# Memory attention of a hybrid encoder layer: three engines in written order, twelve rounds instead of ten

## The chip, the core and the metric

The kernel runs on one core of a Trainium2 chip. The metric is the device time of one execution in microseconds (us). Engines are named as the profile names them: PE (matmuls), DVE (vector), ACT (scalar), POOL (GpSimd) and SP, whose queue issues the DMAs.

## The reference

One encoder layer over 1024 tokens of width 1024. After a norm and one wide projection it has three branches: latent attention with 8 heads ("MLA"), a short convolution, and cross-attention into 256 memory tokens with 4 heads of width 128. Each branch is gated, sent through a matrix, weighted by a sigmoid, and the sum goes through the output matrix. The change is in the third branch alone:

```python
mkv = (rmsnorm(mem, mem_norm_g) @ w_mkv).reshape(B, M, N_HEADS_MEM, 2 * MEM_HEAD_DIM)
m_k, m_v = split_cols(mkv, (MEM_HEAD_DIM, MEM_HEAD_DIM))
mq = rmsnorm(q_mem.reshape(B, S, N_HEADS_MEM, MEM_HEAD_DIM), mem_q_g)
m_k = rmsnorm(m_k, mem_k_g)
s = jnp.einsum('bshd,bmhd->bhsm', mq, m_k).astype(jnp.float32) * (MEM_HEAD_DIM ** -0.5)
p = jax.nn.softmax(s, axis=-1).astype(m_v.dtype)
o_mem = jnp.einsum('bhsm,bmhd->bshd', p, m_v).reshape(B, S, MEM_WIDTH) * jax.nn.silu(g_mem)
```

## The kernel before, in words

Every float32 product is three matmuls: each operand is split into a high and a low part (`mm3`, lines 107 to 111). The wide projection is "dense" work: a generator (`dense`, line 478 on) that issues one matmul per `pull`, 48 for each block of weights, and PE is fed with it wherever a stage would leave PE waiting. A weight block is loaded by SP, split by POOL (`whi` at line 74, `wlo` at line 80) and used by PE. `self.parts` says whether a block is split in one piece or in four quarters that are spread over the 48 pulls of the block before. The dense results go through `sg` (ACT, line 620) and a store `d_r`.

Memory attention (`mem_attn`, line 792 on) goes over 8 blocks of 128 tokens. For a block: `q` projects and normalizes (24 matmuls; `hsq`, `hst`, `qn`), `turn` copies the two 16-bit planes of the result on DVE (`pl`, line 85) and transposes each with a DMA (`plt`, line 86); `qt` puts the planes together again on ACT (`pw`, line 90) and splits into `qh` (ACT) and `ql` (DVE); `sm` computes 12 score matmuls, the maximum (line 830), four exponentials (line 834), the division on POOL (line 836), and turns the probabilities by the same way of planes; `t` puts them together and splits them into `pth` (ACT) and `ptl` (DVE); `o` does the value products of two blocks in two groups of 12 matmuls, multiplies by the gate that a DMA has brought (`gm`, line 861), splits on POOL (`omh`, `oml`) and stores. The tile `gm` has one buffer, so that a gate is loaded only after the split of the gate before.

The MLA loop (`mla`, line 925 on) follows: 64 rounds of scores, maximum (line 957), exponential, planes, transposes, splitting and products, with dense pulls between. There DVE, ACT and POOL run in the order in which the code is written (`manual_schedule`), and so does PE in both stages. In memory attention DVE, ACT and POOL are ordered by the scheduler of the language, which places an instruction by its own estimate of times; SP is ordered so in both stages. The pulls of the MLA loop are what is left up to a fixed total (`r_end - rest - self.pulled`), spread evenly over 70 rounds.

Of the kernel before, what the change touches and what calls it, by code (L numbers as in the profile page):

```python
# [9 lines left out]
F32 = mybir.dt.float32  # L10
F32R = mybir.dt.float32r
# [3 lines left out]
ALU = mybir.AluOpType  # L15
# [3 lines left out]
P = 128  # L19
S = 1024  # L20
D = 1024
TB = S // P
KT = D // P
M = 256
# [3 lines left out]
HM, DM = 4, 128  # L28
EPS = 1e-6
MAGIC = 12582912.0  # L30
NB = 256
# [31 lines left out]
class K:  # L63
# [728 lines left out]
    def mem_attn(self, st, wq, swq):  # L792
        tc, nc, a, d = self.tc, self.nc, self.a, self.d
        v, ps = nc.vector, self.ps
        mt = M // P
        sc = DM ** -0.5
        wk = self.pool(st, "wk3", bufs=2, side="right")
        QN, QT, PR, PT = {}, {}, {}, {}

        def q(tb):  # L800
            ts = slice(tb * P, (tb + 1) * P)
            pq = ps.tile([P, 512], F32, name="mm", bufs=3)
            for kt in range(KT):
                self.mm3(pq, self.hh[:, kt, ts], self.hl[:, kt, ts], wq[0][:, kt, :], wq[1][:, kt, :], kt == 0, kt == KT - 1)
            QN[tb] = wk.tile([P, HM, DM], F32, name="qn", bufs=1)
            self.head_norm(wk, QN[tb], pq.rearrange("p (h d) -> p h d", d=DM), HM, DM)
            QN[tb] = turn(QN[tb].rearrange("p h d -> p (h d)"), 512)

        def turn(x, n):
            pl = wk.tile([P, 2, n], U16, name="pl%d" % n, bufs=1)  # L810
            plt = wk.tile([P, 2, n // P, P], U16, name="plt%d" % n, bufs=1)
            self.planes(x, pl, plt)
            return plt

        def back(plt, n):
            w = wk.tile([P, S // P, P], F32, name="pw", bufs=1)[:, :n // P]
            self.words(w, plt)
            return w

        def qt(tb):  # L820
            QT[tb] = (wk.tile([P, HM, P], F32R, name="qh"), wk.tile([P, HM, P], F32R, name="ql"))
            self.evac(back(QN.pop(tb), 512), *QT[tb], self.mg[:, 0:1])

        def sm(tb):
            qh, ql = QT.pop(tb)
            s = ps.tile([P, HM, M], F32, name="s")
            for h in range(HM):
                self.mm3(s[:, h, :], qh[:, h, :], ql[:, h, :], self.mk[0][:, h, :], self.mk[1][:, h, :], True, True)
            mx = wk.tile([P, 4 * HM], F32, name="mx4", bufs=3)
            v.tensor_reduce(out=mx[:, 0:HM], in_=s, axis=AX.X, op=ALU.max)  # L830
            v.tensor_scalar_mul(mx[:, HM:2 * HM], mx[:, 0:HM], -sc)
            p = wk.tile([P, HM, M], F32, name="p", bufs=2)
            for h in range(HM):
                nc.scalar.activation(out=p[:, h, :], in_=s[:, h, :], func=AF.Exp, scale=sc, bias=mx[:, HM + h:HM + h + 1], accum_out=mx[:, 2 * HM + h:2 * HM + h + 1])
            v.reciprocal(mx[:, 3 * HM:], mx[:, 2 * HM:3 * HM])
            nc.gpsimd.tensor_tensor(out=p, in0=p, in1=mx[:, 3 * HM:].unsqueeze(2).broadcast_to([P, HM, M]), op=ALU.mult)
            PR[tb] = turn(p.rearrange("p h m -> p (h m)"), S)

        def t(tb):
            blk, j = divmod(tb, NB // P)  # L840
            js = slice(j * P, (j + 1) * P)
            w = back(PR.pop(tb), S)
            if j == 0:
                PT[blk] = [[wk.tile([P, 2, mt, NB], F32R, name="pt" + x) for x in "hl"] for _ in range(2)]
            for g in range(2):
                self.evac(w[:, 4 * g:4 * g + 4].rearrange("p (h k) c -> p h k c", h=2), PT[blk][g][0][:, :, :, js], PT[blk][g][1][:, :, :, js])

        def o(blk):
            bs = slice(blk * NB, (blk + 1) * NB)
            pts = PT.pop(blk)  # L850
            for g in range(2):
                gs = slice(2 * g, 2 * g + 2)
                gm = wk.tile([P, 2, NB], F32, name="gm", bufs=1)
                nc.sync.dma_start(gm, d["gm"][:, gs, bs])
                po = ps.tile([P, 2, NB], F32, name="po")
                for hh in range(2):
                    h = 2 * g + hh
                    for k in range(mt):
                        vh, vl = (x[:, k, h * DM:(h + 1) * DM] for x in self.mv)
                        self.mm3(po[:, hh, :], vh, vl, pts[g][0][:, hh, k, :], pts[g][1][:, hh, k, :], k == 0, k == mt - 1)  # L860
                v.tensor_tensor(out=gm, in0=po, in1=gm, op=ALU.mult)
                oh = wk.tile([P, 2, NB], F32R, name="omh", bufs=1)
                ol = wk.tile([P, 2, NB], F32R, name="oml", bufs=1)
                self.split(gm, oh, ol)
                nc.sync.dma_start(d["omh"][:, gs, bs], oh.bitcast(F32))
                nc.sync.dma_start(d["oml"][:, gs, bs], ol.bitcast(F32))
                self.pull(6)

        for i in range(TB + 2):
            n = 8 if i < TB else 16  # L870
            if i < TB:
                q(i)
            if i == TB - 1:
                swq.close()
                self.open_heads()
            if 0 <= i - 1 < TB:
                qt(i - 1)
            if i == TB:
                with tc.issue_after(self.turned):
                    self.load_q(0)  # L880
                    self.load_head(0)
                    self.load_q(1)
            self.pull(n)
            if 0 <= i - 1 < TB:
                sm(i - 1)
            self.pull(n)
            if 0 <= i - 2 < TB:
                t(i - 2)
            self.pull(n)
            if i > 2 and i % 2:  # L890
                o((i - 3) // 2)

    def open_heads(self):
        self.HD = {}
# [306 lines left out]
```

## Time and profile before

| what | before |
|---|---|
| runs, us | 1170.7, 1175.63, 1172.23; median 1172.23 |
| the profiled execution's own time, us | 1169.31 |
| its span from first to last instruction, us | 1167.6 |
| PE busy over the span | 1125.0 us (96%) |
| DVE, ACT, POOL busy over the span | 721.0, 549.3, 565.8 us |
| mean granted clock of PE | 0.993 of full speed |

The times in rows of the trace count from the first instruction of the profiled execution. A row of the timeline gives the start, the duration, engine and line, operation, result<-source and shapes, how many instructions are merged in it (x), and in brackets the idle time of the engine just ahead with what ended it. Matmuls are pipelined, so that the distance between two starts, not the duration, is what one costs. Memory attention runs from 427 to 586 us, the MLA loop from there to 905 us.

### The profile page before, as it was taken

To read this page: it belongs to the slowest core of one execution; us is meant where nothing else is said; L and a number is where in the kernel's file an instruction comes from. 1 tells how busy PE (TensorE), PEld (TensorE's weight loads), DVE (VectorE), ACT (ScalarE), POOL (GpSimd) and SP (SyncE) were. 2 spreads that over 40 slices of the span, in tenths; PEclk is the share of its full clock that TensorE was granted. 3 is DMA by queue.
4 is the path that set the end of the run, shared out by engine and by line. 5 is a ranking of instruction groups with operands and counts; after the bars stand their busy time and mean duration, and the time that the engine had idled before them with its cause. 6 is when DMAs were issued, how large, how long until landed. Compare 5 with 4: busy or idle time off the path is not lost.

```text
span 1167.6 us, 15350 instructions
## 1 busy us (share of the span) xinstructions
PE 1125.0 (96%) x5458; PEld 945.8 (81%) x5458; DVE 721.0 (62%) x1084; ACT 549.3 (47%) x821; POOL 565.8 (48%) x478
## 2 busy tenths in 40 slices
PE   7999999899999999989899999999999999999998
PEld 7998787678888888777778878888888878888887
DVE  6997686343325443556269999999999204656121
ACT  6546575511011105555468878788788302322000
POOL 4456475343324552344447685876785823233200
PEclk8999999999999999999999999999999999999999
DMA  8427999933232333454979999998997598545241
GB/s 297 150 100 178 241 229 250 259 106 107 73 118 81 127 98 101 108 139 114 266 189 222 215 217 216 217 244 204 232 202 161 167 409 304 160 144 173 98 150 49
DMA packets 284589, 207.75 MB, mean 178 GB/s; under 512 B 201632, under 2 KB 253472, under 8 KB 284320
## 3 DMA queue, kind: packets, MB, share of 16 engines
q1 hardware_dynamic: 284512, 206.76, 65.8%
q8 instruction: 43, 0.70, 0.2%
q14 instruction: 34, 0.28, 0.1%
HBM read 108.14 MB, written 50.33 MB: 136 GB/s over the span
## 4 chain that ended last, share of the span: by engine, by line
PE 41%; DVE 22%; DMA 13%; issue 11%; ACT 7%; POOL 4%; SPq 1%; ACTq 0%; DVEq 0%; POOLq 0%
DVE pl L85 8%; PE mm L526 5%; PE mm L530 5%; PE mm L528 5%; DVE mx L957 5%; DMA plt<-pl 5%; PE mm L713 4%; PE mm L715 4%; PE mm L711 4%; PE mm L109 3%; PE mm L110 3%; PE mm L111 3%; DVE ptl L982 2%; PE pm L760 2%; DMA plt<-plq 2%
## 5 line engine op out<-in xcount | busy, mean ns | idle before, releaser
L526 PE MATMUL mm<-hh,whi 128*128 128x512 f32 x672 | 263.7, 392 | 3.5 <-DVE sg L603 3.5
L530 PE MATMUL mm<-hh,wlo 128*128 128x512 f32 x672 | 261.9, 392 | 1.2 <-POOL wlo L80 1.2
L528 PE MATMUL mm<-hl,whi 128*128 128x512 f32 x672 | 262.8, 391 | 0.0
L90 ACT COPY pw<-plt 128x1024 uint16<-128x1024 uint16 (+1 forms) x160 | 198.4, 1305 | 36.5 <-DMA plt<-pl 33.4
L74 POOL TENSOR_SCALAR whi<-wraw 128x256 fp32r<-128x256 f32 (+1 forms) x107 | 107.2, 1002 | 199.5 <-PE pm L760 76.4
L80 POOL TENSOR_TENSOR wlo<-wraw,whi 128x256 fp32r<-128x256 f32 (+1 forms) x108 | 173.5, 1606 | 9.8 <-PE tr L318 1.6
L526 PEld LDWEIGHTS mm<-hh,whi 128*128 128x128 f32 x672 | 126.6, 188 | 30.5 <-DVE sg L603 4.8
L530 PEld LDWEIGHTS mm<-hh,wlo 128*128 128x128 f32 x672 | 126.7, 189 | 27.9 <-POOL wlo L80 1.6
L528 PEld LDWEIGHTS mm<-hl,whi 128*128 128x128 f32 x672 | 126.6, 188 | 25.8
L85 DVE COPY pl<-p 128x1024 uint16<-128x1024 uint16 x144 | 132.7, 961 | 20.0 <-ACT p L960 9.3
L978 POOL TENSOR_SCALAR pth<-pw 128x1024 fp32r<-128x1024 f32 x64 | 80.8, 1262 | 91.2 <-ACT pw L90 91.2
L952 PE MATMUL s<-k,q 96*128 96x512 f32 x384 | 99.5, 394 | 2.3 <-ACT p L960 1.6
L960 ACT ACTIVATE p<-s,mx 128x1024 f32<-128x1024 f32 x64 | 71.5, 1118 | 58.5 <-DVE mx L957 58.3
L982 DVE TENSOR_TENSOR ptl<-pw,pth 128x1024 fp32r<-128x1024 f32 x64 | 94.5, 1477 | 6.8 <-POOL pth L978 6.4
L952 PEld LDWEIGHTS s<-k,q 96*128 96x128 f32 x384 | 71.7, 188 | 20.5 <-ACT p L960 3.1
L957 DVE TENSOR_REDUCE mx<-s 128x1 f32<-128x1024 f32 x64 | 77.2, 1206 | 0.4
L688 ACT ACTIVATE sg<-sg 128x1024 f32<-128x1024 f32 x24 | 25.5, 1062 | 90.1 <-DMA sg<-d_r 88.8
L391 ACT COPY pw<-plt 96x512 uint16<-96x512 uint16 x64 | 43.8, 771 | 27.5 <-DMA plt<-plq 21.8
L620 ACT ACTIVATE sg<-mm,small 128x512 f32<-128x512 f32 x48 | 32.9, 687 | 37.7 <-PE mm L530 25.5
L718 DVE TENSOR_TENSOR acc<-mm,sg 128x512 f32<-128x512 f32 x16 | 10.9, 689 | 52.1 <-PE mm L715 40.3
L76 ACT CAST whi<-wraw 128x1024 fp32r<-128x1024 f32 x9 | 9.5, 1051 | 68.3 <-PE mm L528 66.8
L996 PE MATMUL po<-pth,v 128*128 128x256 f32 x256 | 38.4, 293 | 0.0
(322 smaller groups left out, 2338.5 us busy)
## 6 DMA issues: line engine op xcount, KB each, us to landing
wraw<-in_w_feat SPq DMA_DIRECT2D x48, 512.0 KB, 4.2
d_r<-sg SPq DMA_DIRECT2D x24, 512.0 KB, 3.9
sg<-d_r SPq DMA_DIRECT2D x24, 512.0 KB, 3.8
d_k<-qkt SPq DMA_DIRECT2D x32, 192.0 KB, 3.0
d_q<-qkt SPq DMA_DIRECT2D x32, 192.0 KB, 3.0
q<-d_q SPq DMA_DIRECT2D x32, 192.0 KB, 3.4
wraw<-in_w_br SPq DMA_DIRECT2D x12, 512.0 KB, 4.3
k<-d_k SPq DMA_DIRECT2D x12, 384.0 KB, 5.6
```

Source lines behind the costliest of these rows:

```text
L74: nc.gpsimd.tensor_scalar(out=hi, in0=raw, scalar1=1.0, scalar2=1.0, op0=ALU.mult, op1=ALU.mult)
L80: e.tensor_tensor(out=lo, in0=raw, in1=hi.bitcast(F32), op=ALU.subtract)
L85: self.nc.vector.tensor_copy(pl[:, x], _halves(src, x))
L90: self.nc.scalar.copy(_halves(out, x), plt[:, x])
L526: mm(o, w1, self.hh[:, k, c], start=k == 0, stop=False)
L528: mm(o, w1, self.hl[:, k, c], start=False, stop=False)
L530: mm(o, w2, self.hh[:, k, c], start=False, stop=k == KT - 1)
L952: nc.tensor.matmul(s[:, c], q[:, qi, ts], k[:, ki, c], start=s_, stop=e_)
L957: v.reduce_max(out=mx[:, 1:2], in_=s, axis=AX.X, negate=True)
L960: nc.scalar.activation(out=p, in_=s, func=AF.Exp, bias=mx[:, 1:2], accum_out=mx[:, 2:3])
L978: nc.gpsimd.tensor_scalar(out=parts(i)[0], in0=p, scalar1=1.0, scalar2=1.0, op0=ALU.mult, op1=ALU.mult)
L982: v.tensor_tensor(out=lo, in0=PW.pop(i), in1=hi.bitcast(F32), op=ALU.subtract)
```

## The change

`sm` is divided into `scores` and `soft`, `q` into `q` and `norm`, `o` into `o` and `fin`. Memory attention now fixes DVE, ACT and POOL to written order too, with weight splits in quarters (`self.parts = 4`). A block's scores come two rounds after its projection (before: one), its `t` three (two), and the products of blocks 2b and 2b+1 in round 2b+5 (2b+3), so that 12 rounds stand where 10 stood. `pw` gets a second buffer, `po` a second, `p` loses one. The gate's DMA is written directly ahead of its multiplication instead of ahead of the products. The pulls of the stage are 360 (15 half blocks) instead of 336; the MLA loop gets 24 fewer.

```diff
+        man.enter_context(tc.manual_schedule(engines={E.DVE, E.Activation, E.Pool}))
+        self.parts = 4
...
-            w = wk.tile([P, S // P, P], F32, name="pw", bufs=1)[:, :n // P]
+            w = wk.tile([P, S // P, P], F32, name="pw", bufs=2)[:, :n // P]
...
-            p = wk.tile([P, HM, M], F32, name="p", bufs=2)
+            p = wk.tile([P, HM, M], F32, name="p", bufs=1)
...
+        def o(blk, g):
+            pts = PT[blk]
+            po = ps.tile([P, 2, NB], F32, name="po", bufs=2)
...
+        def fin(blk, g, po):
             bs = slice(blk * NB, (blk + 1) * NB)
...
+            gs = slice(2 * g, 2 * g + 2)
+            gm = wk.tile([P, 2, NB], F32, name="gm", bufs=1)
+            nc.sync.dma_start(gm, d["gm"][:, gs, bs])
+            v.tensor_tensor(out=gm, in0=po, in1=gm, op=ALU.mult)
...
-        for i in range(TB + 2):
-            n = 8 if i < TB else 16
+        LAST = TB + 3
+        for i in range(LAST + 1):
+            n = 8 if i < TB else 14
+            blk = (i - 5) // 2 if i >= 5 and i % 2 else None
+            if 0 <= i - 2 < TB:
+                scores(i - 2)
+                soft(i - 2)
+            self.pull(n)
             if i < TB:
                 q(i)
...
             if 0 <= i - 1 < TB:
                 qt(i - 1)
-            if i == TB:
+            if blk is not None:
+                po = [o(blk, 0)]
+            self.pull(n // 2)
+            if blk is not None:
+                po.append(o(blk, 1))
+            self.pull(n - n // 2)
+            if blk is not None:
+                fin(blk, 0, po[0])
+            if 0 <= i - 3 < TB:
+                t(i - 3)
+            if 0 <= i - 2 < TB:
+                PR[i - 2] = turn(PR[i - 2].rearrange("p h m -> p (h m)"), S)
+            if i < TB:
+                norm(i)
+            if i == TB + 1:
                 with tc.issue_after(self.turned):
                     self.load_q(0)
                     self.load_head(0)
                     self.load_q(1)
             self.pull(n)
-            if 0 <= i - 1 < TB:
-                sm(i - 1)
-            self.pull(n)
-            if 0 <= i - 2 < TB:
-                t(i - 2)
-            self.pull(n)
-            if i > 2 and i % 2:
-                o((i - 3) // 2)
+            if blk is not None:
+                fin(blk, 1, po[1])
+        man.close()
```

Two places where the order moves. The first is DVE in the middle of the stage, in the kernel before: the first two gate multiplications (L861) and what stands around them (L830 maximum, L96 `ptl`, L85 planes, L788 to L790 the norm).

```order
L861 TENSOR_TENSOR gm<-po,gm 128x512
L835 RECIPROCAL mx_4083<-mx_4083 128x4
L99 SCALAR_TENSOR_TENSOR ql<-pw,small,qh 128x512
L85 COPY pl_4093<-p 128x1024 x2
L788 TENSOR_REDUCE hst<-hsq 128x4
L861 TENSOR_TENSOR gm<-po,gm 128x512
L96 TENSOR_TENSOR ptl<-pw,pth 128x4x128
L104 TENSOR_SCALAR hst<-hst 128x4
L96 TENSOR_TENSOR ptl<-pw,pth 128x4x128
L830 TENSOR_REDUCE mx_4254<-s 128x4
L790 TENSOR_TENSOR qn<-mm,hst 128x512
```

The same place in the changed kernel (L840 the maximum, L873 the gate, other lines as before), one whole round from maximum to maximum:

```order
L840 TENSOR_REDUCE mx_4232<-s 128x4
L841 TENSOR_SCALAR mx_4232<-mx_4232 128x4
L845 RECIPROCAL mx_4232<-mx_4232 128x4
L99 SCALAR_TENSOR_TENSOR ql<-pw,small,qh 128x512
L873 TENSOR_TENSOR gm<-po,gm 128x512
L96 TENSOR_TENSOR ptl<-pw,pth 128x4x128 x2
L85 COPY pl_4341<-p 128x1024 x2
L788 TENSOR_REDUCE hst<-hsq 128x4
L104 TENSOR_SCALAR hst<-hst 128x4
L790 TENSOR_TENSOR qn<-mm,hst 128x512
L85 COPY pl_4355<-qn 128x512 x2
L873 TENSOR_TENSOR gm<-po,gm 128x512
```

Every round now has the same sequence: one block's maximum, the next block's `ql`, the previous block's `ptl`, its successor's planes and the newest block's norm follow one another, and the parts of different blocks no longer overtake each other.

The second place is SP's queue at the end of the stage, in the kernel before, from the planes of the second last block of probabilities on (`q`, `k`, `v` are the first loads of the MLA loop):

```order
L86 DMA_TRANSPOSE plt_4675<-pl_4674 128x8x128 x2
L866 DMA d_oml<-oml 128x2x256
L854 DMA gm<-d_gm 128x2x256
L923 DMA q<-d_q 96x2x256
L910 DMA k<-d_k 96x2048
L911 DMA v<-d_v 128x8x128
L923 DMA q<-d_q 96x2x256
```

In the changed kernel, from the planes of the last block on:

```order
L86 DMA_TRANSPOSE plt_4872<-pl_4871 128x8x128
L877 DMA d_omh<-omh 128x2x256
L86 DMA_TRANSPOSE plt_4872<-pl_4871 128x8x128
L878 DMA d_oml<-oml 128x2x256
L949 DMA q<-d_q 96x2x256
L936 DMA k<-d_k 96x2048
L937 DMA v<-d_v 128x8x128
L949 DMA q<-d_q 96x2x256
L872 DMA gm<-d_gm 128x2x256
L622 DMA d_r<-sg 128x1024
L486 DMA wraw<-in_w_feat 128x1024
```

The gate of the second group of blocks 4 and 5 stood ahead of the four MLA loads and now stands behind them; the last transposes stood behind them and now stand ahead. On DVE that gate's multiplication is followed by the last block's `ptl` and then the two gates of blocks 6 and 7, with the MLA loop's first maximum (L983) next:

```order
L873 TENSOR_TENSOR gm<-po,gm 128x512
L96 TENSOR_TENSOR ptl<-pw,pth 128x4x128 x2
L873 TENSOR_TENSOR gm<-po,gm 128x512 x2
L983 TENSOR_REDUCE mx<-s 128x1
L85 COPY pl<-p 128x1024 x2
```

In this sequence the last block's `ptl` comes behind one gate and the MLA loop's first maximum behind two more.

## Rows read from the trace of the kernel before

**Rows 1.** Windows: us; busy us (x) of PE, PEld, DVE, ACT, POOL; clock; DMA share; GB/s
```profile
427.00:586.00 159.00, 147.44 (x722) 122.89 (x720) 77.33 (x114) 78.03 (x145) 65.39 (x46) 0.99 0.55 145
507.00:510.00 3.00, 3.00 (x10) 2.41 (x9) 2.76 (x4) 2.97 (x5) 1.48 (x3) 0.58 0.00 0
```
**Rows 2.** Waits of PE in the stage: total us, times, longest us
```profile
PE s L109 <- ACT qh L98: 3.4, 2, 2.2
PE po L109 <- ACT pth L95: 3.1, 1, 3.1
```
**Rows 3.** Timeline of PE: first and last of 24 projection, of 12 score matmuls
```profile
427.07 0.39 PE L109 MATMUL mm<-wqh,hh 128*128 128x512 f32 x1
...
432.28 0.39 PE L111 MATMUL mm<-wqh,hl 128*128 128x512 f32 x1
...
457.52 0.28 PE L109 MATMUL s<-mkh,qh 128*128 128x256 f32 x1
...
458.82 0.28 PE L111 MATMUL s<-mkh,ql 128*128 128x256 f32 x1
```
**Rows 4.** Timeline of DVE and ACT: the pieces of one block's way
```profile
433.49 0.68 DVE L788 TENSOR_REDUCE hst<-hsq 128x4 f32<-128x512 f32 x1
...
436.23 0.76 DVE L85 COPY pl<-qn 128x512 uint16<-128x512 uint16 x2
...
460.99 0.76 DVE L85 COPY pl<-qn 128x512 uint16<-128x512 uint16 x2
...
468.89 1.28 DVE L85 COPY pl<-p 128x1024 uint16<-128x1024 uint16 x2
...
542.79 2.67 ACT L90 COPY pw<-plt 128x1024 uint16<-128x1024 uint16 x2 [3.83 <-DMA plt<-pl]
...
546.14 1.29 DVE L96 TENSOR_TENSOR ptl<-pw,pth 128x512 fp32r<-128x512 f32 x2 [0.50 <-ACT pth L95]
...
547.61 0.47 ACT L834 ACTIVATE p<-s,mx 128x256 f32<-128x256 f32 x1 [0.40 <-DVE mx L831]
...
549.43 1.42 ACT L90 COPY pw<-plt 128x512 uint16<-128x512 uint16 x2
...
550.88 0.72 ACT L98 ACTIVATE qh<-pw,small 128x512 fp32r<-128x512 f32 x1
```
**Rows 5.** Timeline: planes of a projected block, and when ACT has them back
```profile
532.73 0.75 DVE L85 COPY pl<-qn 128x512 uint16<-128x512 uint16 x2
...
535.71 0.78 ACT L90 COPY pw<-plt 128x512 uint16<-128x512 uint16 x1 [0.25 <-DMA plt<-pl]
```
**Rows 6.** Timeline of POOL and DVE: a weight split beside the plane copies
```profile
537.02 2.38 POOL L80 TENSOR_TENSOR wlo<-wraw,whi 128x1024 fp32r<-128x1024 f32 x1
...
537.10 3.46 DVE L85 COPY pl<-p 128x1024 uint16<-128x1024 uint16 x2 [2.01 <-POOL p L836]
```
**Rows 7.** Timeline: the last two gates, the MLA loop's first scores and maximum
```profile
581.26 0.69 DVE L861 TENSOR_TENSOR gm<-po,gm 128x512 f32<-128x512 f32 x1 [1.06 <-PE po L111]
...
586.21 3.06 PE L952 MATMUL s<-k,q 96*128 96x512 f32 x12 [0.78 <-ACT sg L620]
...
587.48 0.69 DVE L861 TENSOR_TENSOR gm<-po,gm 128x512 f32<-128x512 f32 x1 [5.53 <-DMA gm<-d_gm]
588.09 1.22 DVE L957 TENSOR_REDUCE mx<-s 128x1 f32<-128x1024 f32 x1
```
**Rows 8.** DMA issues from 425 to 592 us: count, KB each, median us to landing
```profile
gm<-d_gm SPq DMA_DIRECT2D x8, 256.0 KB, 3.0
...
v<-d_v SPq DMA_DIRECT2D x2, 512.0 KB, 8.1
```
**Rows 9.** The MLA loop: a window, a DVE group with its idle time, a PE wait
```profile
630.00:870.00 240.00, 235.01 (x1220) 196.70 (x1219) 231.26 (x286) 197.58 (x235) 176.97 (x169) 1.00 0.98 217
...
L957 DVE TENSOR_REDUCE mx<-s 128x1 f32<-128x1024 f32 x47 | 56.7, 1207 | 0.4
...
PE po L993 <- DVE o L1017: 5.5, 9, 1.4
```

More of the change, by code (lines that the diff above doesn't have):

```diff
@@ L797, in mem_attn, with norm @@
         wk = self.pool(st, "wk3", bufs=2, side="right")
-        QN, QT, PR, PT = {}, {}, {}, {}
+        PQ, QN, QT, PR, PT = {}, {}, {}, {}, {}
+        E = mybir.EngineType
+        man = st.enter_context(ExitStack())
+        man.enter_context(tc.manual_schedule(engines={E.DVE, E.Activation, E.Pool}))
+        self.parts = 4
         def q(tb):
             ts = slice(tb * P, (tb + 1) * P)
-            pq = ps.tile([P, 512], F32, name="mm", bufs=3)
+            pq = PQ[tb] = ps.tile([P, 512], F32, name="mm", bufs=3)
             for kt in range(KT):
                 self.mm3(pq, self.hh[:, kt, ts], self.hl[:, kt, ts], wq[0][:, kt, :], wq[1][:, kt, :], kt == 0, kt == KT - 1)
-            QN[tb] = wk.tile([P, HM, DM], F32, name="qn", bufs=1)
-            self.head_norm(wk, QN[tb], pq.rearrange("p (h d) -> p h d", d=DM), HM, DM)
-            QN[tb] = turn(QN[tb].rearrange("p h d -> p (h d)"), 512)
+        def norm(tb):
+            qn = wk.tile([P, HM, DM], F32, name="qn", bufs=1)
+            self.head_norm(wk, qn, PQ.pop(tb).rearrange("p (h d) -> p h d", d=DM), HM, DM)
+            QN[tb] = turn(qn.rearrange("p h d -> p (h d)"), 512)
         def turn(x, n):
@@ L822, in qt, with scores, soft @@
             self.evac(back(QN.pop(tb), 512), *QT[tb], self.mg[:, 0:1])
-        def sm(tb):
+        def scores(tb):
             qh, ql = QT.pop(tb)
-            s = ps.tile([P, HM, M], F32, name="s")
+            s = PR[tb] = ps.tile([P, HM, M], F32, name="s")
             for h in range(HM):
                 self.mm3(s[:, h, :], qh[:, h, :], ql[:, h, :], self.mk[0][:, h, :], self.mk[1][:, h, :], True, True)
+        def soft(tb):
+            s = PR[tb]
             mx = wk.tile([P, 4 * HM], F32, name="mx4", bufs=3)
@@ L836, in sm @@
             nc.gpsimd.tensor_tensor(out=p, in0=p, in1=mx[:, 3 * HM:].unsqueeze(2).broadcast_to([P, HM, M]), op=ALU.mult)
-            PR[tb] = turn(p.rearrange("p h m -> p (h m)"), S)
+            PR[tb] = p
         def t(tb):
@@ L846, in t @@
                 self.evac(w[:, 4 * g:4 * g + 4].rearrange("p (h k) c -> p h k c", h=2), PT[blk][g][0][:, :, :, js], PT[blk][g][1][:, :, :, js])
-        def o(blk):
-            bs = slice(blk * NB, (blk + 1) * NB)
[L850 to L867, printed above, removed]
@@ L869, in mem_attn @@
-        for i in range(TB + 2):
-            n = 8 if i < TB else 16
+        def o(blk, g):
+            pts = PT[blk]
+            po = ps.tile([P, 2, NB], F32, name="po", bufs=2)
+            for hh in range(2):
+                h = 2 * g + hh
+                for k in range(mt):
+                    vh, vl = (x[:, k, h * DM:(h + 1) * DM] for x in self.mv)
+                    self.mm3(po[:, hh, :], vh, vl, pts[g][0][:, hh, k, :], pts[g][1][:, hh, k, :], k == 0, k == mt - 1)
+            return po
@@ new lines, in fin @@
+        def fin(blk, g, po):
+            bs = slice(blk * NB, (blk + 1) * NB)
+            gs = slice(2 * g, 2 * g + 2)
+            gm = wk.tile([P, 2, NB], F32, name="gm", bufs=1)
+            nc.sync.dma_start(gm, d["gm"][:, gs, bs])
+            v.tensor_tensor(out=gm, in0=po, in1=gm, op=ALU.mult)
+            oh = wk.tile([P, 2, NB], F32R, name="omh", bufs=1)
+            ol = wk.tile([P, 2, NB], F32R, name="oml", bufs=1)
+            self.split(gm, oh, ol)
+            nc.sync.dma_start(d["omh"][:, gs, bs], oh.bitcast(F32))
+            nc.sync.dma_start(d["oml"][:, gs, bs], ol.bitcast(F32))
```

## The prediction

> **What bounds the kernel now.** I read the windows first, then PE's waits, then the timeline of the stage. Over the whole kernel PE is the engine that is nearly always busy; the question is where it is not. In memory attention (427 to 586 us) it is busy 147.4 of 159 us [rows 1]: 11.6 us are idle, and its waits name scores that came before `qh` and products that came before `pth` [rows 2]. So this stage is not PE's alone: a block's way over DVE, ACT and the transposes is at times longer than the matmuls that cover it. In the MLA loop both engines are close to full: in 240 us PE is busy 235.0 and DVE 231.3, DVE's maximum, the first thing it does with PE's scores, waits 0.4 us in 47 rounds, and it is PE that waits, 5.5 us in the loop, for DVE to give back the product buffer [rows 9]. There DVE sets the pace.
>
> **PE's work.** One matmul of 512 columns costs (432.28 - 427.07)/23 = 0.227 us, one of 256 columns (458.82 - 457.52)/11 = 0.118 us [rows 3]. The stage gets 24 more pulls: +5.4 us there. The MLA loop loses them, but since DVE does not wait for PE in it [rows 9], shorter matmul time only makes PE wait more. At its ends, where there is no `ptl` yet or no maximum any more, PE gets its share back: 70 rounds lose 24 pulls, 0.34 each, and I count 13 such rounds: 13 x 0.34 x 0.227 = 1.0 us. Bounds: 0 and 5.4. I take 1.0, because the row for the loop shows DVE without a wait for PE.
>
> **The round as it is written now.** The edits of order go together. PE needs 24 + 24 matmuls of 512 columns and 12 of 256 in a middle round, 12.3 us; with two groups of products (rounds 5 and 7) 15.1; round 8 without projection 10.9, rounds 9, 10 and 11: 13.8, 9.5 and 12.4. Rounds 0 and 1 have 10.9 each, so that PE alone could start round 2 at 448.8, round 3 at 461.1, round 5 at 485.7, round 7 at 513.2.
>
> DVE and ACT have a fixed loop of their own. From the end of one block's plane copies: maximum 1.2 us [rows 9], up to 0.4 to the first exponential (I take 0.3), 1.8 for the four of them, 1.45 from putting the planes together to `qh` and 0.7 for `qh`, then 542.79 to 547.43 = 4.6 for the probabilities of the block before up to `ptl`, 1.3 for the next planes, and 433.49 to 436.99 = 3.5 for the norm with its planes [rows 4]. The sum is 14.9 us. The transposes are hidden in it: from the end of the copies (533.48) to the first plane back is 2.2 us [rows 5], and ACT is at its exponentials for 3.3. Two second gates of a pair add 0.7 each, one of them before round 7's norm. So the loop (14.9) is longer than PE's middle rounds (12.3) and about equal to the odd ones (15.1), and the lead of two rounds is used up on the way.
>
> Block 2's copies ended at 461.75 [rows 4]; now eight pulls stand ahead of its projection, 1.8 us, half of it hidden by DVE's queue: 462.6. Block 5's end at 462.6 + 3 x 14.9 = 507.3, block 7's at 462.6 + 5 x 14.9 + 0.7 = 537.8. `ql` comes 6.2 us later (1.2 + 0.3 + 1.8 + 1.45 + 0.7 and as much again). PE reaches block 5's `ql` at 513.5 and it comes at 514.2: a wait of 0.7. Round 8 then starts at 529.0, round 9 at 539.9, and block 7's `ql` comes at 537.8 + 0.7 + 6.2 = 544.7: a wait of 4.5. Rounds 10 and 11 start at 558.2 and 567.7, the stage's last matmul ends at 580.1. Against 585.4 (586.21 less the wait of 0.8 [rows 7], which also stands ahead of the new loop's first scores) that is 5.3 us earlier, with the extra pulls paid: the idle 11.6 us become 5.2, and the half clock (below) is not met.
>
> The quarters of weight splits are hidden: POOL is busy 65 of 159 us [rows 1] and each quarter is written 22 pulls or more ahead of its use. The second `pw` and `po` buffers cost nothing; the single `p` is written again only after the four steps from the copies to the next exponentials, so it makes nothing wait.
>
> [...] The row: beside a weight split of 2.38 us two plane copies that take 1.28 alone took 3.46 [rows 4, 6]. [...] In written order POOL has its quarters ahead of the copies, so I take nothing here and price it as a rival.
>
> **The end of the stage.** Here the gain meets a queue. Block 6's planes are done at 537.8 + 12.1 = 549.9 (the loop without its norm, and one gate), block 7's 9.2 later, at 559.1 (1.2 + 0.3 + 1.8 + 4.6 + 1.3). SP then issues the four MLA loads, and behind them the second gate of blocks 4 and 5, at about 562.5. In the old trace the loads of `v` among them took 8.1 us to land, a gate alone 3.0 [rows 8]: behind them the gate is there at 570.7, multiplied at 571.4, and only then `ptl` of block 7 (1.3), for which PE is ready at 570.9: a wait of 1 to 2, so the last matmul ends near 581.5 and the first MLA scores near 585. The gates then go one by one, each after the split of the one before. From one gate's multiplication to the next with nothing in the way was 587.48 - 581.26 = 6.2, and to the loop's first maximum 0.6 more [rows 7]. With two such steps from 570.7: 583.1, first maximum at 583.7. With the next head's loads in front of the first step (8.1 instead of 3.0): 588.8. I take a value between, 586, since those loads are issued five us ahead of that gate. Now it was 588.09 [rows 7].
>
> **The sum.** First maximum 586 instead of 588.1: -2.1. Pulls that the loop's ends do not need: -1.0. Together -3.1 us. On the profiled execution's 1169.3 that gives 1166.2; this execution lies 2.9 below the median of the runs, so against the median: 1169.1 us. That is 0.3% less, and about 0.5% (5.9 us) is what a measurement here can tell from no change: my forecast is no change that can be told.
>
> **Rival 1, faster.** The gates come early (583.7 or before), or the loop of DVE and ACT is shorter than I add, because instructions overlap by 0.1 us at a dozen places; PE then meets neither wait, and some of the 5.4 us of pulls comes back too. First maximum 583 (-5.1) and 3 us back: -8, that is 1164. For it: PE waits for ACT and DVE in a handful of places only [rows 2], and all have two rounds now. Against: the loop is a chain, and shifting work by a round does not shorten it.
>
> **Rival 2, slower.** POOL is late and its splits meet the copies of the probabilities' planes in each of the five rounds from block 2 to block 7. The price is 3.46 - 1.28 = 2.2 us a round [rows 4, 6], 11 us in all; every later step hangs on block 7, so the time is -3.1 + 11 = +8, or 1180. It decides from 1.8 us a round on. For it: the gate splits now stand in POOL's order ahead of the norm. Against: with the rows' durations POOL has some 2 us of air before the copies.
>
> [...]
>
> That the change does not do what it says is excluded by the order shown: three engines stand as written. SP does not; it stays with the scheduler.
>
> **How the numbers follow.** The forecast, rival 3 included, 0.52; rival 1 0.30; rival 2 0.18. Of the forecast a tenth lies beyond -5.9 (an early gate) and of rival 1 a fifth stays within: faster 0.05 + 0.24 = 0.29 and a little for pulls that come back, 0.31; slower 0.18 and a little for loads still later, 0.20; same 0.49. The forecast's own range: first maximum between 583.7 and 588.8 and pulls back between 0 and 1 give 1166.8 to 1173.1, rounded outward 1166 to 1174. To hold 8 in 10 it must reach into both rivals: 1160 to 1178.
>
> **What the profile will show.** PE's idle time in the stage falls from 11.6 to about 5 us, with its longest wait on `qh` or `ql` in round 9, and few waits on `pth`. The distance of two projected blocks' plane copies in the middle of the stage is near 15 us. The stage's last matmul ends some 5 us earlier, the MLA loop's first maximum less than that, directly behind a gate that DVE waited for. From the first maximum on the loop is as long as before, and PE waits more in it. I am wrong if the first maximum comes 6 us earlier, if the loop gets shorter by the moved pulls, or if plane copies of 2 us and more stand in each round.

## The result, and the profile of the changed kernel

| what | before | changed |
|---|---|---|
| runs, median us | 1172.9 (8 runs) | 1179.08 (8 runs, 1176.14 to 1180.0) |
| ratio | | 1.0051 [1.0035, 1.0068] |
| span of the profiled execution, us | 1167.6 | 1177.6 |
| first maximum of the MLA loop at, us | 588.1 | 597.4 |
| last maximum of the MLA loop at, us | 899.7 | 909.9 |

The change makes the kernel half a per cent slower, where I forecast no change that can be told. The profiled execution of before lies 3.6 us under the median of its eight runs, that of the changed kernel at its median, so the two spans differ by 10.0 us and the medians by 6.2.

The group of the MLA loop's maxima in both kernels, before first (L957, then L983; first and last start):

```profile
L957 DVE TENSOR_REDUCE mx<-s x64: 1196/1205/1225, 588.1 to 899.7; 128x1 f32<-128x1024 f32 x64
```
```profile
L983 DVE TENSOR_REDUCE mx<-s x64: 1194/1204/1226, 597.4 to 909.9; 128x1 f32<-128x1024 f32 x64
```

From first to last maximum it is 311.6 us before and 312.5 now. Of the 10.2 us by which the last maximum is later, 9.3 are there when the loop starts; the 24 pulls taken out of the loop gave back nothing. The window in the loop's middle answers to [rows 9]:

```profile
630.00:870.00 240.00, 232.24 (x1200) 191.96 (x1199) 231.93 (x288) 197.25 (x234) 175.26 (x163) 1.00 0.97 216
```

DVE is as busy as before (231.9 of 240 us), and PE is busy 2.8 us less. PE's waits in the stage, which answer to [rows 2]:

```profile
PE s L109 <- ACT qh L98: 5.3, 2, 3.3
PE po L110 <- DVE ptl L96: 3.3, 1, 3.3
```

They are three, together 8.6 us, where 11.6 us were idle before. Each is followed by half clock: windows of 1 us show 0.50 from 518 to 519, 549 to 550 and 582 to 583 us, and matmuls of 512 columns start 0.43 us apart from 551 to 553, against 0.227. Windows of the stage, and of the stretches behind the three waits (the column after POOL's is the clock):

```profile
427.00:586.00 159.00, 150.38 (x719) 126.93 (x718) 69.89 (x113) 76.91 (x145) 71.16 (x81) 0.96 0.52 132
515.00:520.00 5.00, 3.53 (x14) 3.14 (x15) 1.25 (x2) 4.94 (x8) 4.26 (x5) 0.66 0.11 36
545.00:550.00 5.00, 2.05 (x8) 1.76 (x9) 0.93 (x2) 4.67 (x9) 4.08 (x5) 0.72 0.50 159
550.00:555.00 5.00, 5.00 (x18) 4.15 (x18) 3.38 (x5) 2.07 (x3) 2.98 (x5) 0.59 0.15 36
580.00:585.00 5.00, 3.79 (x15) 3.54 (x16) 2.17 (x3) 0.00 (x0) 4.10 (x6) 0.66 1.06 278
```

Busy time times the share of the clock that is missing gives 1.2 + 0.6 + 2.1 + 1.3 = 5.1 us (rounded terms); the one such stretch of before, in [rows 1], cost 1.3 by the same reckoning. That is a low estimate, since a window's clock is a mean over PE's idle time too (1.00 from 545 to 546 us, where PE is idle, and 0.50 from 549 to 550). By the starts of the matmuls behind the three waits, against 0.227 and 0.118 us for one, it is 1.9 + 3.1 + 1.7 = 6.7 us, and 2.0 in the kernel before. At the end of the stage DVE is last. Its timeline from the last block's planes to the loop's first maximum:

```profile
563.78 2.03 DVE L85 COPY pl<-p 128x1024 uint16<-128x1024 uint16 x2
579.87 0.69 DVE L873 TENSOR_TENSOR gm<-po,gm 128x512 f32<-128x512 f32 x1 [14.06 <-DMA gm<-d_gm]
580.48 1.70 DVE L96 TENSOR_TENSOR ptl<-pw,pth 128x512 fp32r<-128x512 f32 x2
590.52 0.69 DVE L873 TENSOR_TENSOR gm<-po,gm 128x512 f32<-128x512 f32 x1 [8.34 <-DMA gm<-d_gm]
596.74 0.69 DVE L873 TENSOR_TENSOR gm<-po,gm 128x512 f32<-128x512 f32 x1 [5.54 <-DMA gm<-d_gm]
597.35 1.21 DVE L983 TENSOR_REDUCE mx<-s 128x1 f32<-128x1024 f32 x1
```

In the 33 us between the end of those planes (565.8) and the end of the first maximum DVE waits 27.9 us for gates. PE in the same stretch (the last block's first products, the stage's last matmul, the loop's first scores):

```profile
577.62 0.28 PE L109 MATMUL po<-pth,mvh 128*128 128x256 f32 x1
581.22 0.47 PE L110 MATMUL po<-ptl,mvh 128*128 128x256 f32 x1 [3.32 <-DVE ptl L96]
...
591.76 0.39 PE L530 MATMUL mm<-hh,wlo 128*128 128x512 f32 x1
591.99 2.91 PE L978 MATMUL s<-k,q 96*128 96x512 f32 x12
```

The stage's last matmul ends at 592.0, against 585.4 before; 21 pulls stand between the last product and it, where 6 stood before. Where PE is last (e10 below), the maximum starts 1.7 us after the first of these scores. PE alone would thus have let it start at about 593.7 (an estimate), and the gates hold it 3.7 us longer. Through the wait on `ptl` and the half clock behind it the first of them costs PE another 3.3 + 1.7 us. Without both the maximum would come at about 588.7, no earlier than before. Last, SP's queue in the same stretch:

```profile
566.32 0.38 SPq L877 DMA_DIRECT2D d_omh<-omh  x1
566.78 1.29 SPq L86 DMA_TRANSPOSE plt<-pl  x1
568.16 0.54 SPq L878 DMA_DIRECT2D d_oml<-oml  x1
568.79 0.67 SPq L949 DMA_DIRECT2D q<-d_q  x1
569.52 0.57 SPq L936 DMA_DIRECT2D k<-d_k  x1
570.15 0.59 SPq L937 DMA_DIRECT2D v<-d_v  x1
570.78 0.76 SPq L949 DMA_DIRECT2D q<-d_q  x1
571.58 0.72 SPq L872 DMA_DIRECT2D gm<-d_gm  x1
...
574.04 2.69 SPq L936 DMA_DIRECT2D k<-d_k  x1
577.28 0.56 SPq L937 DMA_DIRECT2D v<-d_v  x1
...
583.80 0.63 SPq L872 DMA_DIRECT2D gm<-d_gm  x1
```

The first of these gates is issued at 571.58 behind four MLA loads, and its multiplication starts at 579.87, 8.3 us later; the eight gate loads took 2.8 to 8.2 us to land. Two readings of the 8.2 us are left, the four loads ahead on SP's queue and DMA engines that are merely full (busy share 1.01 from 571.6 to 579.9 us); these runs do not part the two.

### The profile page after: what moved, and what is told of

Same layout as the page of the kernel before. It is cut to its first block, busy times and chain, and to the rows that moved or that the text cites. A ratio compares the mean times of both kernels' runs of the same rounds, so it can differ in the third digit from the quotient of the medians.

```text
span 1177.6 us, 15389 instructions
## 1 busy us (share of the span) xinstructions
PE 1130.6 (96%) x5458; PEld 948.3 (81%) x5458; DVE 712.8 (61%) x1084; ACT 547.5 (46%) x821; POOL 577.3 (49%) x520
## 4 chain that ended last, share of the span: by engine, by line
PE 20%; DVE 15%; DMA 7%; issue 6%; POOL 4%; ACT 2%; SPq 0%; DVEq 0%; ACTq 0%; POOLq 0%
DVE pl L85 7%; DMA plt<-pl 4%; DVE mx L983 4%; PE mm L713 4%; PE mm L715 4%; PE mm L711 4%; DVE ptl L1008 3%; PE mm L110 2%; PE mm L109 2%; PE mm L111 2%; POOL wlo L80 1%; ACT p L986 1%; ACT pw L90 1%; DMA ocl<-d_ocl 1%; POOL whi L74 1%
## 5 line engine op out<-in xcount | busy, mean ns | idle before, releaser
L74 POOL TENSOR_SCALAR whi<-wraw 128x256 fp32r<-128x256 f32 (+1 forms) x128 | 116.7, 912 | 188.7 <-PE pm L760 76.4
L80 POOL TENSOR_TENSOR wlo<-wraw,whi 128x256 fp32r<-128x256 f32 (+1 forms) x129 | 178.4, 1383 | 11.3 <-PE tr L318 1.6
L85 DVE COPY pl<-p 128x1024 uint16<-128x1024 uint16 x144 | 128.0, 929 | 14.0 <-ACT p L986 8.8
L983 DVE TENSOR_REDUCE mx<-s 128x1 f32<-128x1024 f32 x64 | 77.2, 1206 | 0.4
```

The costliest lines, as they stand in the source:

```text
L74: nc.gpsimd.tensor_scalar(out=hi, in0=raw, scalar1=1.0, scalar2=1.0, op0=ALU.mult, op1=ALU.mult)
L80: e.tensor_tensor(out=lo, in0=raw, in1=hi.bitcast(F32), op=ALU.subtract)
L85: self.nc.vector.tensor_copy(pl[:, x], _halves(src, x))
L983: v.reduce_max(out=mx[:, 1:2], in_=s, axis=AX.X, negate=True)
```

## The experiments

Three theories stood against each other. **G**: the gate loads, behind the MLA loads and one by one, hold DVE and so the start of the loop. **P**: the 24 pulls and the clock cost the time. **C**: the fixed order makes a round of DVE and ACT too long (15.5 us). Every experiment is an edit of the changed kernel unless it says otherwise; the ratio is to the kernel before, timed beside it. First and last maximum are those of the MLA loop in the profiled execution. The kernel before had a median of 1172.9 us beside the changed kernel and of 1170.9 to 1171.2 beside the experiments, so that kernels are compared by their ratios and not by their medians. A profiled execution lies up to 3.8 us off the median of its kernel (e9), and what follows the last maximum took 265.5 to 269.8 us in the profiled ones, although the code there is the same.

| run | first maximum | last maximum | median us | ratio |
|---|---|---|---|---|
| changed kernel | 597.4 | 909.9 | 1179.1 | 1.0051 [1.0035, 1.0068] |
| e1 gates early | 588.0 | 908.5 | 1175.8 | 1.0042 [1.0025, 1.0059] |
| e2 MLA loads early | 590.1 | 902.6 | 1173.1 | 1.0014 [0.9997, 1.0030] |
| e3 336 pulls | 595.9 | 907.9 | 1177.4 | 1.0052 [1.0034, 1.0070] |
| e8 gates early, 336 pulls | 585.1 | 907.1 | 1175.6 | 1.0035 [1.0018, 1.0051] |
| e9 two gate buffers | 585.9 | 902.5 | 1174.2 | 1.0023 [1.0009, 1.0037] |
| e10 buffers, loads and pulls | 585.3 | 897.9 | 1165.5 | 0.9950 [0.9933, 0.9967] |
| e6 before, 360 pulls | 589.4 | 900.9 | 1172.0 | 1.0007 [0.9991, 1.0023] |
| e4 without the fixed order | 594.9 | 906.4 | 1176.2 | 1.0049 [1.0031, 1.0067] |
| f1 buffers and loads | 586.8 | 898.3 | 1168.1 | 0.9973 [0.9957, 0.9989] |
| f2 loads and pulls | 591.0 | 903.5 | 1172.4 | 1.0007 [0.9994, 1.0021] |
| f3 before, two gate buffers | 588.1 | 899.5 | 1169.0 | 0.9971 [0.9950, 0.9993] |
| f4 e10, gate after the maximum | 588.2 | 901.8 | 1168.8 | 0.9974 [0.9960, 0.9989] |

**e1, gates early.**

```diff
+            if blk is not None:
+                gate(blk, 0)
+                if blk > 1:
+                    gate(blk, 1)
             if 0 <= i - 2 < TB:
                 scores(i - 2)
...
+            gm = GM[blk, g] = wk.tile([P, 2, NB], F32, name="qn" if g and blk > 1 else "gm", bufs=1)
```

> The changed kernel with its gate loads written at the start of a round of products, and the second gate of the last two pairs in a tile of its own (the idle tile of the norm). Theory G (gates: they are loaded behind the MLA head loads and then one behind the other, and DVE's written order hangs the last ptl and the first MLA maximum on them): DVE's 27.9 us of waits for gates nearly vanish, the wait of 3.3 us on ptl goes, the first MLA maximum comes at 588 to 589 instead of 597.35, the time is 1170 to 1171 us against 1179. Theory P (pulls: the 24 matmuls more in the stage and the clock are what is late, the gates only wait along): only the wait on ptl and its half clock go, about 5 us, 1174. Theory C (chain: the fixed order's round of 15.5 us is what is late): no change, 1178 to 1179.

The first maximum came at 588.0 as G had it, the last `ptl` at 572.8, and PE's wait on it was gone. But the ratio hardly fell (1.0042 against 1.0051). The exponential behind that maximum waited 9.4 us for POOL (timeline of the kernel, from the loop's first maximum to its first exponential):

```profile
587.99 1.23 DVE L993 TENSOR_REDUCE mx<-s 128x1 f32<-128x1024 f32 x1 [0.96 <-PE s L988]
...
594.73 0.62 POOL L74 TENSOR_SCALAR omh<-qn 128x512 fp32r<-128x512 f32 x1 [4.28 <-DMA d_omh<-omh]
595.42 1.26 POOL L80 TENSOR_TENSOR oml<-qn,omh 128x512 fp32r<-128x512 f32 x1
...
596.72 1.11 ACT L996 ACTIVATE p<-s,mx 128x1024 f32<-128x1024 f32 x1 [9.43 <-POOL oml L80]
```

The edit made a wait of its own: the tile that I borrowed for the second gate lies where the loop's first probabilities go (the exponential waited for the split that reads it last), and that split waited for the store of the split before. G was right on the maximum; the run could not price it.

**e2, MLA loads early**, and **e3, 336 pulls.** One line each:

```diff
-            if i == TB + 1:
+            if i == TB:
```
```diff
-            n = 8 if i < TB else 14
+            n = 8 if i < TB else 12
```

> The changed kernel with the four MLA loads one round earlier, where the kernel before has them; the gates stay one by one in one buffer at their use. Theory G: the second gate of blocks 4 and 5 is no longer behind them, it lands at about 572 to 574 instead of 579.8, the last ptl follows at 575, PE does not wait for it; the last two gates still follow one by one, first MLA maximum at 588 to 590, 1170 to 1172 us. If the single buffer alone were the cause, and not the loads ahead: the maximum moves by less than 3 us, 1176 or more. Theory P: 1174. Theory C: 1179.

> The changed kernel with 12 instead of 14 pulls in the half blocks of the last four rounds: 336 pulls in the stage as in the kernel before, the MLA loop gets its 24 back. Theory G: the last gates come as late as now, PE waits where it did its pulls, first MLA maximum within 1.5 us of 597.35, the loop no longer than now or by up to 1 us; 1177 to 1179.5. Theory P: 5.4 us less in the stage and none of it back in the loop, 1173.5 to 1174.5. Theory C: 1178 to 1179.

With the MLA loads a round earlier the gate was multiplied at 573.2 instead of 579.9, PE did not wait for `ptl`, its last product began at 580.2 instead of 587.1, and the first maximum came at 590.1. The time was 1173.1 us, between G (up to 1172) and P (1174); by the ratio the gain is 4 us. So the time does not part the two: the wait on `ptl` and its half clock went, as both had it (the products of 256 columns start 0.12 us apart there, against 0.21 in the changed kernel). Pulls and order are untouched, so neither can be what these 4 us come from. The gates of blocks 6 and 7 still followed one by one (582.0, 589.5).

With 336 pulls the ratio did not fall (1.0052), as G had it; P had some 5 us here, and is out for the pulls. The pulls saved became a wait (PE's waits in the stage):

```profile
PE mm L526 <- POOL whi L74: 9.5, 1, 9.5
```

POOL's next weights stand in its written order behind the split of the late gate: what holds DVE holds POOL too, and PE through it.

**e8, gates as in e1, and 336 pulls.**

> Both: gates early and 336 pulls in the stage. Theory G: with the gates out of the way the end of the stage is PE's, and the pulls of the last rounds count there, while the loop, whose pace DVE sets, takes them for nothing: 3 to 5 us less than with early gates alone, 1165 to 1168. Were PE's matmuls the pace of the loop, they would come back there and the time would be that of early gates alone. Theory P: 1169. Theory C: 1178.

All missed: 1175.6. The first maximum came at 585.1, 3 us ahead of e1, but the wait behind it was longer for it (11.5 us), because it ends with the store of the gate before, as there. The borrowed tile decided.

**e9, two gate buffers**, the clean form of e1, and **e10**, which adds the edits of e2 and e3.

```diff
-            QT[tb] = (wk.tile([P, HM, P], F32R, name="qh"), wk.tile([P, HM, P], F32R, name="ql"))
+            QT[tb] = (wk.tile([P, HM, P], F32R, name="qh", bufs=1), wk.tile([P, HM, P], F32R, name="ql", bufs=1))
...
+            gm = GM[blk, g] = wk.tile([P, 2, NB], F32, name="gm", bufs=2)
```

> The changed kernel with two buffers for the gate, both gates of a round loaded at its start; room comes from qh and ql, which get one buffer each. (The first such run put the second gate into a tile on whose place the MLA loop's first exponential lies.) Theory G, now with what the first four runs show, that the time follows the moment at which the MLA loop gets going, and not the pulls: first maximum at 587.5 to 588.5, nothing waits behind it, so 9 to 10 us earlier than 597.35: 1169.5 to 1171 us. Rival, stores: one buffer for omh and oml makes the splits wait for their stores, and with them POOL's weights or the first exponential: the gain is at most half, 1174 to 1176. Theory C (the round of 15.5 us): 1179.

> Two gate buffers with early loads, MLA loads one round earlier and 336 pulls in the stage, all in one. Theory G: the end of the stage is PE's, the first maximum comes at 582 to 585.5, 1165 to 1168 us: under the kernel before by 3 to 6 us. Rival, loop: PE's matmuls set the loop's pace, the 24 pulls come back there: 1169 to 1171. Rival, stores: 1172 to 1175.

e9 is the rival of the stores: 1174.2. The maximum came at 585.9, but the fourth one at 603.4, since DVE waited for transposes (timeline of the kernel):

```profile
591.83 0.62 POOL L74 TENSOR_SCALAR omh<-gm 128x512 fp32r<-128x512 f32 x1 [4.07 <-DMA d_omh<-omh]
...
592.48 0.36 SPq L883 DMA_DIRECT2D d_omh<-omh  x1
594.17 0.36 SPq L884 DMA_DIRECT2D d_oml<-oml  x1
...
595.91 6.60 SPq L86 DMA_TRANSPOSE plt<-pl  x4
...
602.07 1.29 DVE L85 COPY pl<-p 128x1024 uint16<-128x1024 uint16 x2 [6.18 <-DMA plt<-pl]
```

The store of the first `omh`, issued at 583.46, freed its buffer only at 591.8, while the next head's loads (issued from 576.5 on) filled the DMA engines (busy share 1.02 between 576 and 592 us). The second split waited for it, SP waited for the split, and the loop's first transposes stood in SP's queue behind it. So the gates were one link and the MLA loads beside them another. e10 takes both away: 1165.5, within the range of G, 0.5% under the kernel before. Its first maximum waited 1.6 us for PE's scores, no longer for a gate. Its group of maxima:

```profile
L992 DVE TENSOR_REDUCE mx<-s x64: 1196/1203/1225, 585.3 to 897.9; 128x1 f32<-128x1024 f32 x64
```

312.6 us again, with 24 pulls more in the loop than the changed kernel has.

**e6, the kernel before with 360 pulls** (20 instead of 16 in its last two rounds), and **e4, the changed kernel without `manual_schedule`** in this stage.

> The kernel before with 360 pulls in the stage instead of 336 (20 instead of 16 in the last two rounds), nothing else. If DVE sets the loop's pace, 24 pulls in the stage are not given back in the loop: the loop from first to last maximum stays within 1 us of 311.6, the first maximum comes at 590 to 593.5 instead of 588.1, the time is 1173 to 1176 us against 1171. Rival: they come back in the loop, which is 3 to 5 us shorter: 1170 to 1172.

> The changed kernel without the fixed order of DVE, ACT and POOL: rounds, leads, quarters, buffers and places of the gate loads stay, the scheduler orders the three engines. The last ptl then stands ahead of the three last gates on DVE, but the gates are still loaded behind the MLA loads and one by one. Theory G: the wait on ptl goes, the first maximum still hangs on the last gate, 593 to 597, 1175 to 1178.5 us. Theory C: the fixed order with its round of 15.5 us is what costs, and without it the time is 1173 or less.

e6: the loop kept its length (589.4 to 900.9, 311.5 us), so pulls don't come back in it; but the time rose by 0.8 us only, because the first maximum moved by 1.3. I had missed that 5.4 us of pulls can fill time in which PE waits anyhow. e4: 1176.2, the first maximum at 594.9 behind the last of three gates, as G had it. C falls: the last `ptl` stood ahead of the gates, PE did not wait for it and the maximum came 2.5 us earlier, but the ratio (1.0049) cannot be told from that of the changed kernel.

**f1 to f4.** f1 is e10 with 360 pulls, f2 is e10 without the gate buffers (the gates one by one at their use), f3 is the kernel before with the buffers of e9, and f4 is e10 with

```diff
             if 0 <= i - 2 < TB:
                 scores(i - 2)
                 soft(i - 2)
+            if late:
+                fin(*late)
+                late = None
...
             if blk is not None:
-                fin(blk, 1, po[1])
+                late = (blk, 1, po[1])
+        fin(*late)
```

> Two gate buffers with early loads and MLA loads one round earlier, 360 pulls as in the change: the run that beat both kernels (1165.45) without its cut in pulls. Theory: the MLA loop from first to last maximum stays at 312 to 313 us, the first maximum, here bound by PE, comes 1 to 3 us later than 585.3, the time is 1166.5 to 1169 us. If the pulls came back in the loop, it is 1165 to 1166 with a loop 3 us shorter.

> MLA loads one round earlier and 336 pulls, the gates one by one in one buffer at their use, as in the change. Theory: the last two gates still follow each other by 6 to 8 us each, the first maximum hangs on the last of them at 588 to 590, 1171.5 to 1173.5 us, as with the loads moved alone (1173.1); so the cut in pulls is worth nothing while a gate is last. If PE were last here, 1168 to 1170.

> The kernel before with two gate buffers, room from one buffer each for qh and ql. Theory: its wait of 5.5 us for the last gate goes, but the first MLA scores end only just ahead of it there: first maximum at 587 to 588 instead of 588.1, the time 1169.5 to 1171.5 us, not to be told from 1171. So the order of the change is needed for a gain: PE's last product ends 4 us earlier in it once no gate holds it. If the gate alone were what both kernels lack: 1166 to 1168.

> The run of 1165.45 with the second gate's product and split written behind the next round's maximum and exponentials instead of ahead of them. In the change's trace such a gate takes 0.68 on DVE ahead of the maximum, and beside its split on POOL the 4-column step behind the maximum takes 1.01 instead of 0.17: 1.5 us in two of the rounds. Theory: PE's waits of 6.2 us on qh shrink by 1.5 to 3 us, and the time falls by as much, 1162.5 to 1164.5 us. If the rounds of DVE and ACT are no longer what makes PE late there, no change: 1165 to 1166.

f1: as expected, 1168.1, so the cut in pulls is worth some 2.6 us once PE is last at the stage's end (the two intervals overlap a little). f1 is also the plainest test of G. It keeps the pulls and the written order of the change and moves only the loads and the buffers, and the ratio goes from 1.0051 to 0.9973, 9 us. f2: the time as expected, 1172.4. Its maximum (591.0) came behind PE's scores, because PE had waited 3.3 us for `whi`, whose split stands behind a gate's on POOL. So the cut is worth next to nothing beside e2 while the gates come one by one, and the second buffer is worth 7 us beside e10. f3: 1169.0, a little below what I had; the first maximum at 588.1, where I had 587 to 588, now behind the scores instead of a gate. Up to the last maximum its profile shows no gain over the kernel before (899.5 against 899.7), so where these 2 us are stays open. So a good part of what e10 gains over the kernel before may be had without the change; their intervals overlap. f4 missed: 1168.8. The order did shorten DVE's chain (the 4-column step behind the maximum took 0.17 again, PE's first wait on `qh` fell from 1.95 to 0.56), but in round 9 PE waited 6.2 us. The transposes ahead of that `qh` leave SP one after the other (timeline of the kernel):

```profile
536.42 6.74 SPq L86 DMA_TRANSPOSE plt<-pl  x4
...
545.32 1.38 ACT L90 COPY pw<-plt 128x512 uint16<-128x512 uint16 x2 [1.52 <-DMA plt<-pl]
```

In e10 that copy starts at 545.33 as well: with DVE out of the way the transposes are last there. That f4 is slower than e10 has another place: PE waited 2.1 us for `whi` before 573.84 (0.7 in e10) and then ran at a clock of 0.66 from 575 to 580 us (1.00 in e10).

## Why the prediction was wrong, by its steps

**PE's work: bounds right, price wrong.** I took 1.0 us of the 5.4 as given back by the loop; nothing came back. The reason I gave, that DVE sets the loop's pace, held in every run but e1, e8 and e9, where something at its start waited (311.4 to 313.6 us).

**The loop of DVE and ACT: right in length, late at its start.** From block 2's planes to block 7's I had 5 x 14.9 + 0.7 = 75.2 us; it was 540.65 - 464.95 = 75.7. But I let the loop begin behind block 2, at 462.6. It ran from block 1 on (planes of blocks 1, 2 and 7):

```profile
449.72 0.76 DVE L85 COPY pl<-qn 128x512 uint16<-128x512 uint16 x2
...
463.88 1.07 DVE L85 COPY pl<-qn 128x512 uint16<-128x512 uint16 x2
...
539.89 0.76 DVE L85 COPY pl<-qn 128x512 uint16<-128x512 uint16 x2
```

so that block 7's planes ended 2.85 us later than my 537.8.

**Half clock: the step that I left out of the sum.** The half clock is the stretch with a mean of 0.58 in [rows 1]. The sum has it as not met, and no run shows that term: in the changed kernel it came three times, behind waits of 2.0 to 3.3 us, and cost 5.1 us by the windows, 6.7 by the starts, where the one stretch of before, behind a wait of 2.2 us on `qh` [rows 2], cost 1.3 by the windows. The chances count it, as rival 3, with the forecast; behind round 9's wait of 3.3 us it cost 2.7 by the windows, 3.1 by the starts. Not every such wait was followed by it: in the kernel before PE waited 3.1 us on `pth`, and the clock was 1.00 from 575 to 585 us, around and behind that wait.

**The end of the stage: the step that failed.** I had the mechanism and a date too early. From block 7's projected planes to the planes of its probabilities I had 21.3 us and it was 25.2. Four terms of that way were too small or missing: the 4-column step ahead of the exponentials took 1.00 us instead of 0.17; two dense copies `sg` of 0.7 us stood on ACT ahead of `pth`; the two `ptl` took 2.07 and 1.84 us where I had 1.3; and the plane copy took 2.03 instead of 1.28. SP needed 5.8 us from there to the gate instead of 3.4, because the stores and the second transpose stood between. The landing I had right (8.1, it took 8.2). Together 2.85 + 3.9 + 2.4 = 9.2 us: the gate was multiplied from 579.9 on, not from 570.7. The first step from gate to gate was 10.65 us, with a load beside the next head's `k` and `v` (6.7 us from its issue to the multiplication, DMA busy share 1.04 from 585 to 590 us), the second 6.2 as in [rows 7] (3.0 from issue to multiplication): 17.5 us to the first maximum instead of 15.3. First maximum 597.4 instead of 586: that is the miss.

**The last `ptl`** stands behind that gate on DVE, as I wrote; PE's wait was 3.3 us instead of 1 to 2.

**PE's end was 5 us too early even without that wait.** I had the stage's last matmul end at 580.1, and near 581.5 with the wait on `ptl`; it ended at 592.0. In e2, where PE does not wait for `ptl`, the loop's first scores follow the stage's last matmul at once:

```profile
584.86 0.39 PE L530 MATMUL mm<-hh,wlo 128*128 128x512 f32 x1
585.08 2.91 PE L978 MATMUL s<-k,q 96*128 96x512 f32 x12
```

That is 585.1 against my 580.1. Of the 11.9 us in the changed kernel the half clock has 6.7, the wait on `ptl` 3.3, and 0.9 stand ahead of the stage, which began that much later in this execution. The 5.3 us that PE was to gain were not there: it gained 0.3 in e2. The late gates hid this in the changed kernel; in e1, without them, the maximum waited for PE and came at 588.0, as in the kernel before.

**The rivals.** Rival 2 named 1180, and 1179 came, by another way: plane copies in the middle rounds were not stretched (median 0.684 us each). So the price that I had was met by luck. What the rival stood for was small: beside the split of `oml` the 4-column step took 1.01 and 1.00 us instead of 0.17 in two rounds. Of the range: the slower end (1178) rested on rival 2's price and on the gates at 588.8 at worst; that the gates themselves could make a case on the slower side, with MLA loads ahead of one and beside the next (8.3 and 6.7 us from issue to multiplication, against 3.0 for the third), was missing.

## What to carry to other kernels

Where a later stage runs at the pace of one engine, ask when its first instruction can start: the loop took 311 to 314 us in each of these kernels in which nothing at its start waited, whatever matmuls were moved in or out. Matmuls ahead of it counted only where PE was last at its start (e10 against f1, 2.6 us). The gate loads of the changed kernel, written at their use with one buffer, were issued only after the split of the gate before (583.80, the split until 583.31) and behind what stood ahead on SP's queue (571.58, behind four loads); in the fixed order the wait passed to every engine that had an instruction behind it (27.9 us on DVE for gates, 11.8 on POOL ahead of the first of their splits, 3.3 on PE for `ptl`). Mend such a chain link by link, and look in each run for what is last next: a gate, a tile's place, a store, PE, then a transpose.

## What the runs showed of the hardware

A store of 256 KB took 2.4 us to land in the median of this stage before (`omh`), and over 8 us in e9, where the DMA engines' busy share was 1.02 from 576 to 592 us: there the buffer of a store was the slowest part of the chain. The transposes of one round, four of them, held SP for 6.7 us (536.42 to 543.16 in f4); I had not counted SP as an engine that can be last. A wait of PE of 2.0 us was followed by half clock (0.50 from 518 to 519 us, 0.66 from 515 to 520, in the changed kernel), one of 3.1 us in the kernel before was not (1.00 from 580 to 585).
